# GpSimd's gate multiplications, lower parts of weights and update of x issued in pieces of 256 columns, in a two-layer token-mixer and PEER decoder on one core

## The chip, the cores and the metric

The program runs on one core of a Trainium2 chip. A core has TensorE (matrix products; PE in the profile, its weight loads PEld), VectorE (DVE), ScalarE (ACT), GpSimd (POOL) and SyncE (SP), which here issues most of the loads from device memory. Every engine works through its own list in order; semaphores tie the lists together. The metric is the device time of one execution in microseconds.

## The reference, cut to what matters

Two layers over 256 tokens of 1024 channels in float32. Each has a token mixer and a feed-forward part of single-neuron experts; both end in `layer_norm(ALPHA * x + y)`.

```python
for l in range(DEPTH):
    sh1, sc1, gt1, sh2, sc2, gt2 = jnp.split(cond @ w_ada[l] + b_ada[l], 6, axis=-1)
    hm = x * (1.0 + sc1[:, None]) + sh1[:, None]
    proj = hm @ w_in[l]                  # nine parts: q, f, i, g; q, k, v; two gates
    oa = hgrn2_chunkwise(...)            # then head norm and silu gate
    ob = stick_breaking_attention(...)
    merged = sigmoid(gate_a) * (oa @ w_up_a[l]) + sigmoid(gate_b) * (ob @ w_up_b[l])
    y = (merged @ w_o[l]) * gt1[:, None]
    x = layer_norm(DN_ALPHA * x + y, ln_g[l, 0], ln_b[l, 0])
    hf = x * (1.0 + sc2[:, None]) + sh2[:, None]
    y = peer_ffn(hf, w_pq[l], sub_keys[l], peer_u[l], peer_v[l]) * gt2[:, None]
    x = layer_norm(DN_ALPHA * x + y, ln_g[l, 1], ln_b[l, 1])
```

## The kernel before

Every float32 product is made of three products of rounded halves: a weight W is loaded into a buffer `raw` (128 x 1024, one of five), ScalarE writes its rounded upper part (tile `wh`, L58), and VectorE or GpSimd the lower part, raw minus upper part (tile `wl`, L271). TensorE forms upper x upper, upper x lower, lower x upper (L61). One load of weights is two halves of 512 columns, so two upper and two lower parts. A `raw` buffer is loaded again when its lower parts are made.

The loads stand in one list, `order`, in the order of their use, with a kind each: "w" (input and up projections), "o" (rows of w_o), "q" (queries), "u" and "x" (experts' first weights), "v" (their second). `take` fetches the next load and has one prepared ahead (`prep`); in the mixers two. Which engine makes a lower part: for u and x GpSimd; for q, and for loads prepared during a layer norm, GpSimd too (`pool_lo`); for w and o in the mixers the function `lighter`, which keeps a sum of work for each of the two engines (`load`) and gives the part to the one with less; else VectorE. Operations that GpSimd does besides are added to the sum by hand.

A mixer goes through these steps. The projections: TensorE works through w_in; between two loads a generator (`pull`) issues a piece of the side work, first `decays`, then `hgrn`, then `stick`. `hgrn` builds the scores of the HGRN2 recurrence by a binary tree of levels: for each, two subtractions on VectorE give exponents (L843, L844, tile `e`), ScalarE takes the exponential in place, two multiplications on VectorE (L856, L857, tile `qk`) give scaled keys and queries, TensorE multiplies them (tiles `hs`, `ss`), and a predicated copy (L887) places the scores. Then the second half, called the merge below: four times two up-projections on TensorE, whose results VectorE multiplies by the gates and adds (L1281 to L1283, tile `gel`), and the rows of w_o, which GpSimd multiplies by the row gt1 (tile `gt_row`, L223) when their load is near, before they are split into upper and lower part. As slabs for these parts serve tiles that the projections no longer need, so parts of w_o carry names such as `qT`, `kk`, `gaT`, `qk`. The layer norm and the first loads of the next stage follow.

In layer 1 the side work has one more member, `update_x`: x was left without the scale and shift of the last layer norm, and GpSimd applies them (L698 and L702) while the projections run. In the expert stage the same is done for the other norm, in sixteen operations of 256 columns in blocks (L1737).

Of the kernel before, what the change touches and what calls it, by code (L numbers as in the profile page):

```python
# [8 lines left out]
F32 = mybir.dt.float32  # L9
# [36 lines left out]
def trunk_kernel(ctx: ExitStack, tc: tile.TileContext, x, c, w_ada, b_ada, w_in, lb_logits, hg_norm_g,  # L46
                 w_up_a, w_up_b, w_o, w_pq, sub_keys, peer_u, peer_v, ln_g, ln_b, out):
    nc = tc.nc
# [8 lines left out]
    def act(o, i, f, **kw):  # L57
        nc.scalar.activation(o, i, f, **kw)  # L58
# [143 lines left out]
    state = {}  # L202
    xt = [const.tile([P, D], F32, name=f"x{tt}") for tt in range(2)]
    live, used = [], []
    load = {"vector": 0.0, "pool": 0.0}

    def lighter(vector, pool):

        if load["pool"] + pool < load["vector"] + vector:
            load["pool"] += pool  # L210
            return nc.gpsimd
        load["vector"] += vector
        return nc.vector

    def turn(n):

        for i in range(min(n, len(fetched))):
            kind, t = fetched[i]
            if kind == "u":
                nc.vector.transpose(t, t)  # L220
                fetched[i] = ("ut", t)
            elif kind == "o" and state.get("gt_row") is not None:
                nc.gpsimd.tensor_mul(t, t, state["gt_row"])  # L223
                load["pool"] += 2.4
                fetched[i] = ("ot", t)

    def prep():


        turn(1)  # L230
        kind, t = fetched[0]
        kind = kind[0]
        if kind in "mk":
            fetched.popleft()
            prepped.append((kind, t, None, None))
            return True
        place = room_for(kind)
        if not place:
            return False
        fetched.popleft()  # L240
        live.append(place)
        hs, ls = [], []
        if kind == "v" and state.get("vprep"):
            state["vprep"]()
        banks = []
        if kind == "x":

            for s in range(2):
                banks.append(pst.tile([P, 4, P], F32, name="T"))
                for q in range(4):  # L250
                    nc.tensor.transpose(banks[s][:, q], t[:, (4 * s + q) * P:(4 * s + q + 1) * P], ident)  # L251
        for s in range(2):
            h = place.tile([P, 512], F32R, name="wh")
            lo = place.tile([P, 512], F32R, name="wl")
            hs.append(h)
            ls.append(lo)
            if kind == "u":
                src = t.rearrange("p (a k r) -> p a k r", a=4, k=KC)[:, :, 4 * s:4 * s + 4]
                h, lo = (a.rearrange("p (k a r) -> p a k r", k=4, a=4) for a in (h, lo))
            else:  # L260
                src = t[:, s * 512:(s + 1) * 512]
            if kind == "x":
                act(h, banks[s].rearrange("p k r -> p (k r)"), AF.Copy)
                act(src, banks[s].rearrange("p k r -> p (k r)"), AF.Copy)
            else:
                act(h, src, AF.Copy)
            if kind in "ux" or state.get("pool_lo"):
                eng = nc.vector if s and state.get("share_lo") else nc.gpsimd
            else:
                eng = lighter(0.6, 1.0) if kind == "o" or kind == "w" and not state.get("slab") else nc.vector  # L270
            eng.tensor_sub(lo, src, h.bitcast(F32))  # L271
        h, lo = halves(hs), halves(ls)
        prepped.append((kind, h, lo, place))
        return True
# [10 lines left out]
    def room_for(kind):  # L285


        more = [state["more"]] if state.get("more") and not live.count(state["more"]) else []
        if kind == "w" and more:
            return more[0]  # L290
        if state.get("slab"):
            slab = state["slab"](kind)
            if slab:
                return slab
        if kind == "o" and more:
            return more[0]
        return hlp if live.count(hlp) < HALVES // 2 else None

    def halves(tiles):
        return lambda sl: tiles[sl.start // 512][:, sl.start % 512:(sl.stop - 1) % 512 + 1]  # L300

    def take(kind):
        if state.get("skip"):
            state["skip"] -= 1
        else:
            fetch()
        if kind not in "mk":
            for e in load:
                load[e] = max(0.0, load[e] - STEP)
        while used and not state.get("hold"):  # L310
            live.remove(used.pop())
        if not prepped:
            prep()
        k, h, lo, place = prepped.popleft()
        assert k == kind, (k, kind)
        if place:
            used.append(place)
        while state.get("ahead", True) and fetched and sum(p[0] not in "mk" for p in prepped) < state.get("depth", 1):
            if not prep():
                break  # L320
        turn(1 if kind in "ux" else 3)
        return h, lo
# [110 lines left out]
    def load_row(dst, src):  # L433
        nc.gpsimd.dma_start(dst, bass.AP(tensor=src.tensor, offset=src.offset, ap=[[0, P], [1, D]]))
# [36 lines left out]
    class Ahead:  # L471
# [27 lines left out]
        def others(self):  # L499

            self.tile(1, loads=range(2))
            for _ in range(2):
                live.remove(used.pop(-3))
            state["hold"] = False
            while prep():
                pass
            self.tile(1, loads=range(2, 4))
# [148 lines left out]
    def mixers(l, hT):  # L656
        with ExitStack() as es:
            ap = es.enter_context(tc.tile_pool(name=f"at{l}", bufs=1))
            psj = es.enter_context(tc.tile_pool(name=f"psj{l}", bufs=4, space=PSUM))
            gt_row = ap.tile([P, D], F32, name="gt_row")  # L660
# [29 lines left out]
            def update_x():  # L690

                g_row = ap.tile([P, D], F32, name="mh0")
                b_row = ap.tile([P, D], F32, name="mh1")
                load_row(g_row, ln_g[l - 1, 1])
                load_row(b_row, ln_b[l - 1, 1])
                yield None
                for tt in range(2):
                    nc.gpsimd.tensor_mul(xt[tt], xt[tt], g_row)  # L698
                    load["pool"] += 2.4
                    yield None  # L700
                    yield None
                    nc.gpsimd.tensor_add(xt[tt], xt[tt], b_row)  # L702
                    load["pool"] += 2.4
                    yield None
                    yield None

            if l == 0:
# [517 lines left out]
            if l:  # L1225
                sides.append(update_x())
# [35 lines left out]
            for i in range(4):  # L1262
                pp = []
                for oh, ol, n in ((oah, oal, "T"), (obh, obl, "A")):
                    h, lo = take("w")
# [529 lines left out]
```

## Time and profile before

| | |
|---|---|
| median of 3 runs | 2228.16 us (2227.01 to 2228.52) |
| the profiled execution | 2227.97 us, its span 2226.2 us |
| TensorE busy | 2117.0 us, 95% |
| VectorE busy | 1819.4 us, 82% |
| ScalarE busy | 1164.5 us, 52% |
| GpSimd busy | 1063.8 us, 48% |
| mean granted TensorE clock | 0.985 |

Busy shares are averages over the whole span. Each layer has a mixer (0 to about 310 us, 1123 to about 1400 us), the experts' first weights (to 770 and 1862 us) and the experts' second weights. A time in the rows below is counted from the start of the span.

### The profile page before, as it was taken

How to read it: one execution, taken by the hardware profiler on the slowest of the kernel's cores; microseconds unless marked ns; L12 is line 12 of the kernel's file. 1: busy time of each engine (PE TensorE's matmuls, PEld its weight loads, DVE VectorE, ACT ScalarE, POOL GpSimd, SP SyncE). 2: the span in 40 equal slices, each digit the busy share in tenths (PEclk: the TensorE clock that was granted, in tenths of full speed). 3: DMA queues.
4: the chain of work that ended last, by engine and by line, in shares of the span. 5: the costliest groups of instructions: out<-in, count | busy, mean ns of one | idle time of the engine just before them, and what ended most of it. 6: DMA issues, size and time to landing. Idle time of an engine off the chain costs nothing.

```text
span 2226.2 us, 42039 instructions
## 1 busy us (share of the span) xinstructions
PE 2117.0 (95%) x14484; PEld 1928.0 (87%) x14484; DVE 1819.4 (82%) x3296; ACT 1164.5 (52%) x2443; POOL 1063.8 (48%) x784
## 2 busy tenths in 40 slices
PE   5799899999999999999989998998999999999998
PEld 5789799999999977888779887998999999788886
DVE  7887979999999578888887658789999985766675
ACT  3446555545554545555545465555555545555562
POOL 4656637887778621000044534578877783300001
PEclk8899999999999999999999999999999999999999
DMA  8646567676665678888844335676766556666662
GB/s 281 193 133 221 167 132 158 149 151 146 143 147 146 186 251 270 282 283 284 298 153 146 120 103 146 149 155 142 154 146 145 147 159 192 220 196 191 197 226 87
DMA packets 448718, 400.30 MB, mean 180 GB/s; under 512 B 234576, under 2 KB 395896, under 8 KB 448504
## 3 DMA queue, kind: packets, MB, share of 16 engines
q1 hardware_dynamic: 446760, 392.33, 62.5%
q0 software_dynamic: 1408, 4.23, 0.6%
q8 instruction: 114, 1.87, 0.3%
q10 hardware_dynamic: 336, 1.06, 0.1%
q14 instruction: 100, 0.82, 0.1%
HBM read 396.46 MB, written 1.05 MB: 179 GB/s over the span
## 4 chain that ended last, share of the span: by engine, by line
PE 69%; DVE 15%; DMA 5%; issue 3%; ACT 3%; POOL 2%; SPq 1%; POOLq 0%; ACTq 0%; DVEq 0%
PE Y L61 27%; PE A L61 25%; PE T L61 7%; PE G L61 3%; DMA raw<-in_peer_u_dram 3%; POOL wl L271 2%; PE hs L61 2%; DVE wl L271 2%; PE ss L61 2%; PE T L251 2%; DMA raw<-in_peer_v_dram 1%; DVE qk L857 1%; DVE o L1512 1%; SPq L197 1%; DVE e L843 1%
## 5 line engine op out<-in xcount | busy, mean ns | idle before, releaser
L271 POOL TENSOR_TENSOR wl<-raw,wh 128x512 fp32r<-128x512 f32 x663 | 925.7, 1421 | 662.0 <-ACT wh L58 587.3
L58 ACT ACTIVATE wh<-raw 128x512 fp32r<-128x512 f32 x1088 | 627.7, 622 | 206.8 <-PE A L61 59.0
L61 PE MATMUL A<-hTh,wh 128*128 128x256 f32 x2080 | 538.5, 291 | 2.7 <-ACT wh L58 2.6
L61 PE MATMUL A<-hTl,wh 128*128 128x256 f32 x2080 | 521.0, 283 | 0.0
L61 PE MATMUL Y<-wh,o 128*128 128x512 f32 x1776 | 478.1, 391 | 0.5 <-DVE o L521 0.5
L271 DVE TENSOR_TENSOR wl<-raw,wh 128x512 fp32r<-128x512 f32 x525 | 379.7, 764 | 64.0 <-ACT wh L58 46.4
L61 PEld LDWEIGHTS A<-hTh,wh 128*128 128x128 f32 x2080 | 397.8, 191 | 4.7 <-ACT wh L58 4.0
L61 PEld LDWEIGHTS A<-hTl,wh 128*128 128x128 f32 x2080 | 398.7, 192 | 0.7
L61 PEld LDWEIGHTS Y<-wh,o 128*128 128x128 f32 x1776 | 332.6, 188 | 70.0 <-DVE o L521 0.9
L61 PE MATMUL A<-hTh,wl 128*128 128x256 f32 x2080 | 336.2, 284 | 13.5 <-POOL wl L271 13.4
L61 PEld LDWEIGHTS A<-hTh,wl 128*128 128x128 f32 x2080 | 286.9, 192 | 17.6 <-POOL wl L271 17.6
L61 PE MATMUL Y<-wl,o 128*128 128x512 f32 x888 | 276.3, 391 | 5.2 <-DVE wl L271 5.0
L220 DVE STREAM_TRANSPOSE raw<-raw 128x1024 f32<-128x1024 f32 x206 | 252.8, 1233 | 3.2 <-DMA raw<-in_peer_u_dram 2.7
L58 ACT ACTIVATE o<-buf 128x256 fp32r<-128x256 f32 x228 | 95.0, 417 | 272.6 <-PE Y L61 272.6
L521 DVE TENSOR_TENSOR o<-buf,o 128x256 fp32r<-128x256 f32 x228 | 100.7, 442 | 140.2 <-ACT o L58 140.2
L61 PEld LDWEIGHTS Y<-wl,o 128*128 128x128 f32 x888 | 167.1, 188 | 44.0 <-DVE wl L271 9.5
L58 ACT ACTIVATE buf<-G 128x128 f32<-128x128 f32 (+6 forms) x236 | 53.8, 273 | 202.7 <-PE G L61 202.7
L1507 DVE TENSOR_TENSOR o<-iT,iota_t 128x1024 f16<-128x1024 f16 x128 | 159.5, 1246 | 0.0
L570 POOL TENSOR_TENSOR x<-x,buf 128x1024 f32<-128x1024 f32 x1 | 2.4, 2392 | 280.9 <-DVE x L567 280.9
L1512 DVE TENSOR_TENSOR o<-gT,o 128x1024 f16<-128x1024 f16 x128 | 131.3, 1025 | 4.4
L61 PE MATMUL T<-hTh,wh 128*128 128x256 f32 x512 | 133.8, 293 | 0.0
L61 PE MATMUL T<-hTl,wh 128*128 128x256 f32 x512 | 130.4, 287 | 0.0
(496 smaller groups left out, 3212.6 us busy)
## 6 DMA issues: line engine op xcount, KB each, us to landing
raw<-in_peer_u_dram SPq DMA_DIRECT2D x1024, 128.0 KB, 3.5
raw<-in_peer_v_dram SPq DMA_DIRECT2D x256, 512.0 KB, 4.6
raw<-in_w_in_dram SPq DMA_DIRECT2D x88, 512.0 KB, 4.7
raw<-in_w_ada_dram SPq DMA_DIRECT2D x78, 512.0 KB, 4.9
raw<-in_w_o_dram SPq DMA_DIRECT2D x16, 512.0 KB, 3.5
raw<-in_w_pq_dram SPq DMA_DIRECT2D x64, 128.0 KB, 2.9
qk<-in_w_ada_dram SPq DMA_DIRECT2D x10, 512.0 KB, 3.7
e<-in_w_ada_dram SPq DMA_DIRECT2D x8, 512.0 KB, 6.0
```

The source lines that it names most:

```text
L58: nc.scalar.activation(o, i, f, **kw)
L61: nc.tensor.matmul(o, a, b, start=start, stop=stop, **kw)
L197: nc.sync.dma_start(dst[32 * b:32 * b + 32], src[b])
L220: nc.vector.transpose(t, t)
L251: nc.tensor.transpose(banks[s][:, q], t[:, (4 * s + q) * P:(4 * s + q + 1) * P], ident)
L271: eng.tensor_sub(lo, src, h.bitcast(F32))
L521: nc.vector.tensor_sub(lo, src, h.bitcast(F32))
L570: nc.gpsimd.tensor_mul(xt[tt], xt[tt], last[0])
L843: eng.tensor_sub(ev[:, :, :hn], mid, bv[:, :, :hn])
L857: nc.vector.tensor_mul(tv[:, :, hn:], nodes(qT, n)[:, :, hn:], ev[:, :, hn:])
L1507: nc.vector.tensor_tensor(o.rearrange("p a u n v -> p (a u) n v"), iT[:, b].rearrange("p a (u v) -> p (a u) v", v=2)[:, :, None] .to_broad ...
L1512: nc.vector.tensor_mul(og.rearrange("p u a n v -> p (u a) n v"), gT[:, b * nu:(b + 1) * nu].rearrange("p u a v -> p (u a) v")[:, :, None] ...
```

## The change

It issues three kinds of GpSimd operations in pieces of 256 columns, and changes the numbers by which they enter the balance:

```diff
             elif kind == "o" and state.get("gt_row") is not None:
-                nc.gpsimd.tensor_mul(t, t, state["gt_row"])
-                load["pool"] += 2.4
+                for c in range(0, 1024, 256):
+                    nc.gpsimd.tensor_mul(t[:, c:c + 256], t[:, c:c + 256], state["gt_row"][:, c:c + 256])
+                load["pool"] += 2.9
...
-            eng.tensor_sub(lo, src, h.bitcast(F32))
+            if kind not in "ux" and eng is nc.gpsimd:
+
+                for c in (slice(0, 256), slice(256, 512)):
+                    eng.tensor_sub(lo[:, c], src[:, c], h[:, c].bitcast(F32))
+            else:
+                eng.tensor_sub(lo, src, h.bitcast(F32))
...
-                for tt in range(2):
-                    nc.gpsimd.tensor_mul(xt[tt], xt[tt], g_row)
-                    load["pool"] += 2.4
-                    yield None
-                    yield None
-                    nc.gpsimd.tensor_add(xt[tt], xt[tt], b_row)
-                    load["pool"] += 2.4
-                    yield None
+                for n in range(16):
+                    cs = slice(n % 4 * 256, n % 4 * 256 + 256)
+                    xc = xt[n // 8][:, cs]
+                    (nc.gpsimd.tensor_add if n // 4 % 2 else nc.gpsimd.tensor_mul)(
+                        xc, xc, (b_row if n // 4 % 2 else g_row)[:, cs])
+                    load["pool"] += 0.7
                     yield None
```

A lower part becomes two operations, a gate multiplication four, and the four operations of `update_x` sixteen, one for each pull, where before one operation had two pulls. The lower parts of u and x stay whole. Lists of TensorE, ScalarE and SyncE are the same as before.

GpSimd, merge of layer 0, before (`raw<-raw,gt_row` is a gate multiplication, the others are lower parts of w_o):

```order
L223 TENSOR_TENSOR raw<-raw,gt_row 128x1024
L271 TENSOR_TENSOR qT<-raw,qT 128x512
L223 TENSOR_TENSOR raw<-raw,gt_row 128x1024
L271 TENSOR_TENSOR kbT<-raw,kbT 128x512
L223 TENSOR_TENSOR raw<-raw,gt_row 128x1024
L271 TENSOR_TENSOR v_b<-raw,v_b 128x512
L223 TENSOR_TENSOR raw<-raw,gt_row 128x1024 x2
L271 TENSOR_TENSOR bb<-raw,bb 128x512
L223 TENSOR_TENSOR raw<-raw,gt_row 128x1024 x3
L271 TENSOR_TENSOR qk<-raw,qk 128x512
L271 TENSOR_TENSOR wl<-raw,wh 128x512
```

The same place in the changed kernel (its lines are up to six further down):

```order
L224 TENSOR_TENSOR raw<-raw,gt_row 128x256 x4
L275 TENSOR_TENSOR qT<-raw,qT 128x256 x2
L224 TENSOR_TENSOR raw<-raw,gt_row 128x256 x4
L275 TENSOR_TENSOR kbT<-raw,kbT 128x256 x2
L224 TENSOR_TENSOR raw<-raw,gt_row 128x256 x4
L275 TENSOR_TENSOR v_b<-raw,v_b 128x256 x2
L224 TENSOR_TENSOR raw<-raw,gt_row 128x256 x12
L275 TENSOR_TENSOR sc_2490<-raw,sc_2490 128x256 x2
L224 TENSOR_TENSOR raw<-raw,gt_row 128x256 x8
L275 TENSOR_TENSOR wl<-raw,wh 128x256 x2
```

Besides the sizes, the lower parts `bb` and `qk` have gone to VectorE and `sc` has come to GpSimd; layer 1 reads the same.

GpSimd, layer 1, where the tree begins (the two MEMSETs clear its score tiles; `x_80<-x_80,mh` is the update of x by the shift row), in the changed kernel:

```order
L829 MEMSET sc_14493 128x1024
L830 MEMSET sc_14494 128x512
L275 TENSOR_TENSOR wl<-raw,wh 128x256 x4
L706 TENSOR_TENSOR x_80<-x_80,mh_13988 128x256
L275 TENSOR_TENSOR wl<-raw,wh 128x256 x2
L706 TENSOR_TENSOR x_80<-x_80,mh_13988 128x256
L275 TENSOR_TENSOR wl<-raw,wh 128x256 x4
L706 TENSOR_TENSOR x_80<-x_80,mh_13988 128x256
L275 TENSOR_TENSOR wl<-raw,wh 128x256 x4
L706 TENSOR_TENSOR x_80<-x_80,mh_13988 128x256
L275 TENSOR_TENSOR wl<-raw,wh 128x256 x72
```

Before, the four updates stood ahead of the MEMSETs, and 43 lower parts of 512 columns followed them without a break. Ahead of this place VectorE has four lower parts less in layer 1 and GpSimd four more.

## Rows read from the trace of the kernel before

**Rows 1.** Windows: length, busy us (x instructions) of PE, PEld, DVE, ACT, POOL.

```profile
80.00:235.00 155.00, 142.17 (x1005) 130.13 (x1003) 120.46 (x129) 85.06 (x147) 101.60 (x69) 0.97 0.58 185
235.00:285.00 50.00, 43.77 (x260) 38.24 (x261) 47.67 (x57) 26.72 (x47) 27.61 (x13) 0.90 0.54 153
...
1160.00:1335.00 175.00, 162.47 (x1211) 152.16 (x1211) 113.07 (x153) 92.59 (x161) 86.82 (x62) 0.98 0.41 127
1335.00:1390.00 55.00, 47.31 (x267) 40.64 (x266) 49.38 (x63) 28.81 (x54) 26.38 (x15) 0.94 0.58 151
```

**Rows 2.** Chain that ended last, one level in layer 1: start, us, what.

```profile
1225.26 1.79 DVE qk L857
1227.05 1.68 DVE e L843
1228.73 0.61 DVE e L844
...
1229.43 1.07 ACT e L58
...
1231.13 1.79 DVE qk L857
```

**Rows 3.** Waits, 112 to 152 us, then 1212 to 1252 us: total, times, longest.

```profile
PE hs L61 <- DVE qk L857: 4.4, 5, 1.3
...
PE hs L61 <- DVE qk L857: 5.8, 6, 1.1
```

**Rows 4.** Line L857: durations in ns, least, median, most.

```profile
L857 DVE TENSOR_TENSOR qk<-qT,e x16: 679/1788/1802, 109.0 to 1248.7; 128x512 f32<-128x512 f32 x16
```

**Rows 5.** Timeline of GpSimd: start, us, operation.

```profile
279.73 1.37 POOL L271 TENSOR_TENSOR wl<-raw,wh 128x512 fp32r<-128x512 f32 x1 [0.32 <-POOL qk L271]
...
295.04 1.30 POOL L271 TENSOR_TENSOR qbT<-raw,qbT 128x512 fp32r<-128x512 f32 x1
...
1225.22 2.96 POOL L271 TENSOR_TENSOR wl<-raw,wh 128x512 fp32r<-128x512 f32 x2 [2.90 <-ACT wh L58]
```

**Rows 6.** Lines L223 and L1737: durations in ns, first and last start.

```profile
L223 POOL TENSOR_TENSOR raw<-raw,gt_row x16: 2378/2760/2871, 232.3 to 1363.6; 128x1024 f32<-128x1024 f32 x16
...
L1737 POOL TENSOR_TENSOR x<-x,buf x32: 709/916/1717, 822.0 to 1929.0; 128x256 f32<-128x256 f32 x32
```

**Rows 7.** Timeline, merge of layer 1.

```profile
1341.22 2.38 POOL L223 TENSOR_TENSOR raw<-raw,gt_row 128x1024 f32<-128x1024 f32 x1
1341.26 2.89 DVE L1283 TENSOR_TENSOR gel<-gel,mgb 128x512 f32<-128x512 f32 x1
```

**Rows 8.** Groups by form, VectorE, 239.5 to 281 and 1335 to 1376 us.

```profile
L271 DVE TENSOR_TENSOR wl<-raw,wh 128x512 fp32r<-128x512 f32 x13 | 18.9, 1498 | 0.3 <-ACT wh L58 0.3
L1283 DVE TENSOR_TENSOR gel<-gel,mgb 128x512 f32<-128x512 f32 x4 | 4.8, 1191 | 0.1
...
L271 DVE TENSOR_TENSOR wl<-raw,wh 128x512 fp32r<-128x512 f32 x12 | 14.2, 1226 | 0.0
L1283 DVE TENSOR_TENSOR gel<-gel,mgb 128x512 f32<-128x512 f32 x4 | 8.1, 2014 | 0.1
```

**Rows 9.** Waits of TensorE, 239 to 282 us, then 1333 to 1377 us.

```profile
PE T L61 <- DVE wl L271: 2.4, 2, 1.8
...
PE T L61 <- DVE wl L271: 4.9, 2, 2.8
```

**Rows 10.** Timeline of VectorE beside the 256-column updates, expert stage of layer 0.

```profile
832.73 1.22 DVE L271 TENSOR_TENSOR wl<-raw,wh 128x512 fp32r<-128x512 f32 x1
```

**Rows 11.** Timeline, start of layer 0: GpSimd, then VectorE.

```profile
54.50 6.34 POOL L271 TENSOR_TENSOR wl<-raw,wh 128x512 fp32r<-128x512 f32 x5
...
54.59 1.26 DVE L682 TENSOR_SCALAR m_a<-iota_f,part_f 128x8 f32<-128x8 f32 x1
```

**Rows 12.** Timeline, expert stage of layer 0: VectorE, then GpSimd.

```profile
821.02 4.26 DVE L271 TENSOR_TENSOR wl<-raw,wh 128x512 fp32r<-128x512 f32 x2
...
821.96 2.77 POOL L1737 TENSOR_TENSOR x<-x,buf 128x256 f32<-128x256 f32 x4
```

## The prediction

> **What bounds the kernel now.** I looked first at the stretches. Outside the start and the token mixers TensorE hardly stops; in the mixers it does. The four rows of [rows 1] are the two halves of each layer's mixer: TensorE is idle for 155.0 − 142.2 = 12.8 us and 50.0 − 43.8 = 6.2 us in layer 0, 175.0 − 162.5 = 12.5 us and 55.0 − 47.3 = 7.7 us in layer 1. Of the change's parts nearly all stand there (the parts of the expert weights, kinds u and x, keep their 512 columns), so about 39 us of idle TensorE is what there is to win, and a longer VectorE or GpSimd path is what there is to lose.
>
> Next the chain of waits. In the first half it runs through VectorE level after level of the HGRN2 tree: [rows 2] is one level, 5.87 us from one multiplication L857 to the next, of which ScalarE's exponential has 1.07 and VectorE the rest. TensorE waits for that L857: 4.4 us over levels in layer 0, 5.8 us in layer 1 [rows 3]. Why VectorE is slow there shows in the durations: L857 takes 679 ns at its shortest and 1788 ns as a rule [rows 4]. It starts at 1225.26; GpSimd started a pair of lower parts at 1225.22 [rows 5]. The first 512 columns of GpSimd hold L857 for 1.79 − 0.68 = 1.11 us; the second half of the pair holds L843, which takes 1.68 us of the chain where the unheld L844 takes 0.61, so 1.07 us. The two engines take turns: GpSimd, VectorE, GpSimd, VectorE.
>
> In the second half (up-projections, merge, w_o) the longest holders are the multiplications by the gate row: 2378 ns at their shortest [rows 6], and a VectorE operation that comes 0.04 us behind one takes 2.89 us [rows 7]. There VectorE's lower parts and the last addition of the merge are on average far above 0.68 us [rows 8], and TensorE waits for its lower parts for 2.4 us in layer 0 and 4.9 us in layer 1 [rows 9].
>
> **The price of a piece.** The trace has the new form already: the update of x in the expert stage is issued in 256 columns. Alone it takes 0.709 us [rows 6]; its median beside VectorE's lower parts is 0.916, and a 512-column operation of VectorE that meets one takes 1.22 us [rows 10], which is a whole turn of both engines. So a piece holds VectorE for 1.22 − 0.68 = 0.54 us where 512 columns hold it for 1.1 and 1024 for 2.2. Undisturbed, a pair of pieces costs GpSimd 2 × 0.71 = 1.42 us against 1.30 for 512 columns [rows 5]; I take 0.12 us as what one more instruction costs. The changed program has 173 lower parts in 350 pieces, 16 gate multiplications in 64 and 4 updates of x in 16, 237 instructions more, so some 28 us more of GpSimd, spread over an engine that is idle more than half of the time.
>
> A rule that speaks against the change: the Trainium skill, GPSIMD Engine Reference, section 2.1, says that every GpSimd instruction passes a dispatch in software first, tens of cycles. The 0.12 us of the rows is of that size; an estimate by the page's 1.2 GHz, with 100 cycles for its tens, is 20 us for the 237, no more than by the rows.
>
> **Levels of the tree.** In a level where VectorE then waits for the exponential, L857, L843 and L844 now meet one piece each, 3 × 0.54 = 1.62 us instead of 1.11 + 1.07 = 2.18; the fourth piece runs while VectorE waits for ScalarE. That is 0.56 us a level. By the chain ten levels end that way, four in layer 0 and six in layer 1: 5.6 us. Four others in layer 0 have further VectorE work behind L844 (accumulating weights, reducing); there all four pieces are paid, 4 × 0.54 = 2.16 for 2.18, nothing. The last level of each layer is held once before TensorE's products: 2 × (1.11 − 0.54) = 1.1 us. TensorE's waits of 4.4 and 5.8 us have room for it.
>
> Against it: the update of x in layer 1 went out in four operations before the tree; now the last four of its sixteen pieces stand between the tree's first lower parts. Each can hold VectorE once more: nothing to 2.2 us. I take half, −1.1, since two of them fall behind L844, where VectorE waits for ScalarE anyway. Levels together: +5.6 us (bounds +2 to +8).
>
> **Merge.** Each of the four waits of [rows 9] (2.4 us in two, the longer 1.8; 4.9 in two, the longer 2.8) stands behind a hold by a whole gate multiplication, 2.2 us; held by a piece it is 0.54, so each can shrink by 1.67: 1.67 + 0.6 in layer 0, 1.67 + 1.67 in layer 1, 5.6 us. What comes back: the balancing gives VectorE one lower part more in each layer (two gained, one lost), 2 × 0.61; and the last lower part on GpSimd, which the last w_o products need, comes in two pieces, 2 × 0.2. Left: about +4 us. The bounds are wide. VectorE's whole excess over 0.68 us is 13 × 0.82 + 4 × 0.51 = 12.7 us in layer 0 and 12 × 0.55 + 4 × 1.33 = 11.9 in layer 1 [rows 8], yet TensorE's idle time caps it at 6.2 and 7.7; from the other side a multiplication whose four pieces all collide takes 4 × 1.22 = 4.9 us against the median 2.76 [rows 6], and ScalarE's rounding of w_o waits for it. So −5 to +9, and I stay near the middle, by the waits that the rows show.
>
> **Start of layer 0, and the hand-overs.** Here I expect nothing. At 54.5 us five lower parts follow each other and hold five small VectorE operations, each 1.2 to 1.3 us instead of 0.2 [rows 11]. In pieces they hold ten by half as much, and the VectorE work behind is long enough to meet all ten. The same holds for the decays around 92 us. GpSimd's later end delays a buffer's release by one 0.12 us. Bounds −1 to +1.
>
> **Sum.** 5.6 + 4 − 0.1 = 9.5 us off the profiled execution's 2227.97 us, which is 0.2 us below the median of the runs (2228.16): 2218.5 us.
>
> **Rivals.** *The port time is the same.* GpSimd holds VectorE for a time that goes by the columns it works on, and they are as many as before. Where VectorE has enough work behind the first held operation, as in [rows 11], it pays every column anyway. If that held in the ten levels and the merge too, only the two last levels would gain, 1.1 us, less the 1.2 of the extra lower parts: 2228 us, no change. The Trainium skill, SBUF — State Buffer, "two separate sides", states the mechanism: an exclusive lock, held for a whole instruction; the trace agrees in that L857 waits for the end of an operation, 1.11 us. Against the rival: VectorE's pause for ScalarE in each level, 1.07 us, in which a piece costs nothing. Chance 0.2.
>
> *GpSimd becomes the bound of the merge (slower).* In layer 0 its first gate multiplication begins at 232.3 us [rows 6] and its last lower part ends at 281.1 [rows 5]; into these 49 us go 32 + 18 = 50 pieces, 35.5 us alone and 0.51 more for each that collides (1.22 less 0.71). From 27 collisions on GpSimd would be late, from 32 on by more than the levels bring (2.8 us a layer); VectorE has about 30 lower parts, last additions and the like there that can be held. At 40 it is late by 7 us a layer: 14 less 5.6, 2236 us. For it: w_o's rounding waits for the multiplications. Against: GpSimd is idle half of these stretches [rows 1]. Chance 0.1.
>
> *VectorE isn't let in between pieces (slower).* Once a VectorE lower part stayed out until four pieces had passed one behind the other: two of them took 4.26 us where 1.28 would do, with 2.77 us of pieces beside it [rows 12]. In the levels four pieces in one block hold L857 for 2.8 us instead of two holds of 2.18 together, 0.6 × 10 = 6 us, and the merge brings nothing: 2234 us. Against: that one came right behind a DMA issue of GpSimd, and [rows 10] shows the engines taking turns on the same form a dozen us later. Chance 0.05.
>
> *More than forecast.* If the merge gives back two thirds of TensorE's 13.9 idle us there, 9.3, and the pieces of x cost nothing: 2212 us. Chance 0.2. The forecast itself, 2214 to 2222, has 0.45.
>
> **Numbers.** A measurement of this kernel tells about 0.2%, 4.5 us, from no change. Faster by more: 0.45 + 0.2 = 0.65; within: 0.2; slower: 0.15. The range reaches over the first rival and the start of the slower ones and down past the larger gain: 2208 to 2232, which leaves out some 0.1 above and 0.05 below.
>
> **What would show it.** Right: L857, L843 and L844 at about 1.2 us each in place of 1.79, 1.75 and 0.68, the levels some 5.3 us apart, TensorE's wait for L857 about halved; no VectorE operation of the merge above about 1.4 us; gate pieces between 0.7 and 1.2 us. Wrong: levels still 5.87 us apart (the port's time is the same); VectorE operations of 2.5 us and more beside rows of pieces (not let in); ScalarE's rounding of w_o or TensorE's products waiting for gate pieces (GpSimd the bound). What would make the number wrong though the mechanism is right is the merge, whose term has the widest bounds.

## The result, and the profile after

The changed kernel takes 2213.11 us (median of 4 runs, 2211.72 to 2214.66) against 2227.75 us for the kernel before on the same chip (4 runs): a ratio of 0.9934, 95% interval 0.9917 to 0.9952, so 14.6 us off with some 4 us either way. The forecast was 9.5 us off. The profiled execution has a span of 2210.5 us against 2226.2, 15.7 us less.

The engines' busy time on the page, to be read beside the table of before: TensorE does the same work, GpSimd 91 us more where the working had some 28, VectorE 39 us less (a held operation counts as busy for as long as it is held).

```profile
PE 2116.5 (96%) x14484; PEld 1925.0 (87%) x14484; DVE 1780.7 (81%) x3294; ACT 1164.5 (53%) x2443; POOL 1155.3 (52%) x1021
```

A level of layer 1's tree in the timeline of the changed kernel, VectorE and then GpSimd (start us, us, operation), the answer to [rows 2, 5]:

```profile
1211.95 0.69 DVE L860 TENSOR_TENSOR qk<-kk,e 128x512 f32<-128x512 f32 x1 [0.49 <-ACT e L58]
1212.57 1.25 DVE L861 TENSOR_TENSOR qk<-qT,e 128x512 f32<-128x512 f32 x1
1213.74 1.21 DVE L847 TENSOR_TENSOR e<-bb 128x512 f32<-128x512 f32 x1
1214.87 1.21 DVE L848 TENSOR_TENSOR e<-bb 128x512 f32<-128x512 f32 x1
...
1217.27 0.69 DVE L860 TENSOR_TENSOR qk<-kk,e 128x512 f32<-128x512 f32 x1 [0.50 <-ACT e L58]
...
1212.52 4.16 POOL L275 TENSOR_TENSOR wl<-raw,wh 128x256 fp32r<-128x256 f32 x4 [0.46 <-ACT wh L58]
```

Four pieces begin at 1212.52. Three VectorE operations meet one each, 1.25, 1.21 and 1.21 us; the fourth piece runs while VectorE waits for the exponential. The levels are 1217.27 − 1211.95 = 5.32 us apart instead of 5.87. TensorE's waits for the second multiplication, over levels in layer 0 and in layer 1 (total, times, longest), against 4.4 and 5.8 us in [rows 3]:

```profile
PE hs L61 <- DVE qk L861: 1.6, 3, 0.7
...
PE hs L61 <- DVE qk L861: 2.6, 5, 0.6
```

The gate pieces, least, median and most in ns, beside the whole ones of [rows 6]:

```profile
L224 POOL TENSOR_TENSOR raw<-raw,gt_row x64: 718/1183/1266, 226.7 to 1356.0; 128x256 f32<-128x256 f32 x64
```

In the merges VectorE's lower parts are now at 1.03 us instead of 1.50 in layer 0 [rows 8], and none of its operations takes above 1.24 us:

```profile
L277 DVE TENSOR_TENSOR wl<-raw,wh 128x512 fp32r<-128x512 f32 x17 | 16.9, 1033 | 2.7 <-ACT wh L58 2.6
L527 DVE TENSOR_TENSOR acc<-gel,mh 128x512 fp32r<-128x512 f32 x4 | 4.8, 1198 | 0.7 <-ACT mh L58 0.7
```

**Where the time came from.** TensorE's list is the same in all these kernels, 14,484 products, so the n-th product of one trace can be set beside the n-th of another. The table gives how many us earlier than before TensorE leaves a stretch, less how many it entered it earlier; the stretches are bounded by the products that start nearest behind 80, 232, 300, 1124, 1150, 1172, 1255, 1335 and 1390 us in the trace of before. The first column counts from the start of the span, the last is the whole up to the last product. The lines behind the first are the experiments below.

```
                               start layer0 merge0 experts norm masks tree1 stick1 merge1 rest   all
                                0-80 80-232    -300  -1124 -1150 -1172 -1255 -1335  -1390
changed kernel                  1.8    4.3    0.7    2.2    0.9   2.5   3.0  -0.2   -0.1   0.5  15.7
e1 lower parts alone            1.1    4.3    0.8    0.6    1.2   0.3   4.9   0.0   -0.8  -0.2  12.2
e2 gates alone                 -0.8    0.1    1.0    0.6    0.0   0.0  -0.9   0.0    2.6   0.2   2.9
e3 update of x alone           -0.4   -0.5    0.7    0.5    0.0   0.4  -3.3   0.0    0.0   0.3  -2.2
e4 all but the gates            1.9    3.7    0.7    3.0    1.2   2.3   3.3   0.0    0.0   0.8  16.9
e5 w_o's lower parts on DVE     0.9    4.3    3.0    2.3    0.9   2.8   4.0  -0.4    1.7   0.6  20.2
e5b w_o's lower parts whole     1.9    4.0    1.6    0.7    0.9   3.5   4.0  -0.2    1.5   0.8  18.6
e6 lower parts in 128           4.0   -8.0   -0.9    1.8    1.5   5.4  -0.7  -0.5   -2.2   0.6   1.3
e7 row loads by SyncE           1.2    4.2    0.2    1.5    0.9   1.6   2.0  -0.2   -0.7   0.7  11.3
e8 as e5, gates whole           0.9    4.0    0.6    2.1    1.1   2.3   3.3  -1.9    1.7   0.8  15.0
e9 as e5, gates on DVE          0.7    4.3    5.4    3.2    1.2   2.7   2.7  -0.3    4.6   0.6  25.2
e10 gates on DVE, parts shared  1.5    4.1    4.0    2.7    1.2   2.7   2.6  -0.3    2.7   0.6  21.9
e11 as e9, all parts on DVE     1.6   -2.0    2.4    1.4    1.2   5.0   2.8   0.0    4.4   0.5  17.2
```

Where two kernels have the same instructions in a stretch, the column shows the scatter of one execution: e2 and e3 differ from before by up to 0.8 us at the start, the kernels with lower parts in pieces lie between 0.6 and 3.2 us over the 820 us of the experts. Nor do the other columns repeat to a tenth: e1 and e4, alike in all of layer 0, differ by 0.6 us in its tree, and e3, which is the kernel before in all of layer 0, shows 0.7 us in its merge. So a difference below 1 us says little by itself, and in the experts' column one of 2.4 says nothing.

The merges are the surprise: of the 15.7 us, they hold 0.6 us, and the 0.7 of layer 0 is no more than e3 shows there without a change. TensorE is 10.9 us early by 274 us, against 6.1 us where the merge begins, and has given 4.1 of the 4.8 us back by 300 us; in layer 1 it gains 5.7 us and gives 5.8 back. The end of the merge of layer 0 in the timeline of the changed kernel, GpSimd and then ScalarE:

```profile
266.37 6.47 POOL L224 TENSOR_TENSOR raw<-raw,gt_row 128x256 f32<-128x256 f32 x6
273.58 1.87 POOL L275 TENSOR_TENSOR wl<-raw,wh 128x256 fp32r<-128x256 f32 x2 [0.74 <-ACT wh L58]
...
270.60 0.63 ACT L58 ACTIVATE wh<-raw 128x512 fp32r<-128x512 f32 x1 [1.64 <-POOL raw L224]
272.87 2.71 ACT L58 ACTIVATE wh<-raw 128x512 fp32r<-128x512 f32 x5 [1.64 <-POOL raw L224]
```

GpSimd works on gate pieces up to 272.84; ScalarE rounds the last rows of w_o when they are through, and TensorE's last products need these. ScalarE's waits for gate multiplications over this merge (230 to 277 us: total, times, longest) add up to 7.7 us; in the kernel before they are 0.2 us:

```profile
ACT wh L58 <- POOL raw L224: 3.3, 2, 1.6
...
ACT sc L58 <- POOL raw L224: 1.6, 1, 1.6
ACT gaT L58 <- POOL raw L224: 1.4, 1, 1.4
ACT v_b L58 <- POOL raw L224: 0.8, 1, 0.8
ACT e L58 <- POOL raw L224: 0.6, 1, 0.6
```

### The profile page after: what moved, and what is told of

It reads as the page before. It is cut to its first block, busy times and chain, and to the rows that moved or that the text cites. A ratio compares the mean times of both kernels' runs of the same rounds, so it can differ in the third digit from the quotient of the medians.

```text
span 2210.5 us, 42352 instructions
## 1 busy us (share of the span) xinstructions
PE 2116.5 (96%) x14484; PEld 1925.0 (87%) x14484; DVE 1780.7 (81%) x3294; ACT 1164.5 (53%) x2443; POOL 1155.3 (52%) x1021
## 5 line engine op out<-in xcount | busy, mean ns | idle before, releaser
L277 POOL TENSOR_TENSOR wl<-raw,wh 128x512 fp32r<-128x512 f32 x512 | 713.5, 1420 | 199.7 <-ACT wh L58 135.5
L275 POOL TENSOR_TENSOR wl<-raw,wh 128x256 fp32r<-128x256 f32 x310 | 272.7, 912 | 388.2 <-ACT wh L58 382.8
L277 DVE TENSOR_TENSOR wl<-raw,wh 128x512 fp32r<-128x512 f32 x521 | 371.2, 752 | 73.1 <-ACT wh L58 55.0
```

The costliest lines, as they stand in the source:

```text
L275: eng.tensor_sub(lo[:, c], src[:, c], h[:, c].bitcast(F32))
```

## The experiments

The theory after the two traces: a GpSimd operation keeps VectorE out for its own length; pieces halve that wherever VectorE has a short chain, in the start, the norms and the masks too, not in the trees alone; in the merges GpSimd itself becomes what TensorE waits for. The rivals: the gain outside the trees is the scatter of one execution; the merges end where they do for another reason (loads, or the sum of both engines' work).

**e1 to e3, one part alone; e4, all but the gates.** Each is the kernel before with the named parts of the diff: e1 the lower parts, e2 the gate multiplications (with the 2.9), e3 the update of x, e4 the lower parts and the update of x. The kernel before was measured again beside each group of experiments; its medians lie between 2227.06 and 2228.45 us, so medians of different groups can be compared to some 1.4 us.

> Only the lower parts in pieces; gate multiplications and the update of x whole, as before. Theory 1 (every VectorE operation that a lower part holds is held half as long, in the trees and in the start, the masks and the layer norms too): TensorE comes out of the two trees 4.3 and 3.1 us earlier or a little more, out of the start some 1.8 us earlier, out of the experts' hand-overs and the layer norm ahead of layer 1 some 2 to 3 us earlier; about 11 us off in all. Theory 2 (as forecast: only the trees gain, and what the changed kernel shows at the start and the hand-overs is the scatter of one profiled execution): 6 to 7 us off.

Measured: 2215.13 us (5 runs), ratio 0.9944 (0.9930 to 0.9958), 12.6 us off. The first theory holds: start, norm and tree of layer 1 gain 1.1, 1.2 and 4.9 us.

> Only the gate multiplications in pieces. Only the two merges can differ. Theory 1 (GpSimd is the bound of the end of the merge: in the changed kernel it works without a pause from 249.3 to 272.8 us, a gate multiplication in four pieces takes 4.7 us instead of 2.85, and the last roundings of w_o wait for it): TensorE is some 4 us earlier in the middle of each merge and has given nearly all of it back at its end; 0 to 2 us off in all. Theory 2 (as forecast, each wait for a lower part behind a gate multiplication shrinks and the end follows): 4 us off.

Measured: 2223.35 us (11 runs), ratio 0.9982 (0.9973 to 0.9991), 4.4 us off. Here the forecast's 4 us stand, and the first theory's "0 to 2" does not: alone, the gate pieces bring 1.0 and 2.6 us in the two merges (of the 1.0, e3's 0.7 may be scatter). It was too coarse: what the gates bring depends on whether GpSimd's lower parts are in pieces as well.

> Only the update of x in layer 1 in sixteen pieces. Theory 1 (the whole operations hold the small mask operations of VectorE for about 2.2 us each, and these stand in one chain ahead of the lower parts that TensorE waits for; the pieces go elsewhere): TensorE's wait for VectorE's lower part at the masks shrinks from 4.9 us by 1.5 to 2.5 us, the pieces that fall into the tree take back up to 1 us; 1 to 2 us off. Theory 2 (as forecast): nothing gained at the masks, the tree some 1 us longer; 1 us slower.

Measured: 2231.22 us (11 runs), ratio 1.0014 (1.0005 to 1.0023), 3.5 us slower. Neither size is right; the direction is the forecast's. Beside whole lower parts nearly nothing is gained at the masks (0.4 us), and the pieces that fall into the tree cost 3.3 us.

> Lower parts and the update of x in pieces, the gate multiplications whole: the changed kernel less its gate pieces. Theory 1 (the gate pieces give back at the merge's end what they gain in its middle): as fast as the changed kernel within 1.5 us, 13 to 16 us off the kernel before. Theory 2 (as forecast, the gate pieces bring 4 us): 9 to 11 us off.

Measured: 2211.58 us (5 runs), ratio 0.9928 (0.9915 to 0.9942), 16.1 us off, as fast as the changed kernel or a little faster. Given the other two parts, the gate pieces bring nothing. In e4 ScalarE waits for no gate multiplication, but TensorE waits 4.6 us for VectorE's lower parts (230 to 280 us), which are held by whole multiplications again: one wait in the place of the other. From e1 to e4 the update of x in pieces brings 2.0 us at the masks and costs 1.6 in the tree; the rest of what lies between their traces stands mostly in start and experts of layer 0, where the two kernels have the same instructions. Scatter of one execution is not all of it, though: their medians are 3.5 us apart, and each run of e4 is faster than each of e1. What the rest is stays open.

**e5, e5b, e8: who is the bound of the merge.** In e5 GpSimd makes no lower part of a gated row of w_o; in e5b it makes them whole; e8 is e5 with the gate multiplications whole.

```diff
-                eng = lighter(0.6, 1.0) if kind == "o" or kind == "w" and not state.get("slab") else nc.vector
+                eng = nc.vector if kind == "o" and state.get("gt_row") is not None else lighter(0.6, 1.0) if kind == "o" or kind == "w" and not state.get("slab") else nc.vector
```

```diff
-            if kind not in "ux" and eng is nc.gpsimd:
+            if kind not in "uxo" and eng is nc.gpsimd:
```

> The changed kernel, but VectorE makes all lower parts of w_o behind the gate multiplications, GpSimd has only the gate pieces there. Theory 1 (GpSimd's row of pieces is what the end of the merge waits for: in the changed kernel ScalarE waits 7.7 us for gate pieces in the merge of layer 0): that wait falls to 3 us or less, the 4.1 and 5.8 us that TensorE gives back at the two merge ends become 1 to 2, and the kernel is 2 to 6 us faster than the changed one, about 2209 us. Theory 2 (the two engines share one path to the buffers, and the sum of their work bounds the merge, whoever does it): VectorE's five lower parts more in each layer, at 0.68 us, come in the place of GpSimd's, and nothing is gained: 2213 us within 1.5.

Measured: 2206.35 us (4 runs), ratio 0.9907 (0.9892 to 0.9922), 6.8 us faster than the changed kernel, somewhat more than the first theory's 2 to 6. The five lower parts are dearer on GpSimd than on VectorE. At their ends the merges give back 1.0 us in layer 0, as expected, but 2.7 in layer 1; ScalarE's waits for gate pieces fall to 3.9 us, a little more than expected.

> The changed kernel, but the lower parts of w_o on GpSimd whole (512 columns), the gate multiplications in pieces. With whole lower parts everywhere the gate pieces alone brought TensorE 1.0 us in the merge of layer 0 and 2.6 us in that of layer 1; in the changed kernel the merges brought 0.7 and nothing. Theory 1 (each collision of a piece with a VectorE operation costs GpSimd 0.5 us, and five lower parts in ten pieces make it late by some 2 us at the end of each merge): the merges as with the gate pieces alone, 2 to 3 us faster than the changed kernel, about 2211 us. Theory 2 (the difference is scatter of one execution): as the changed kernel, 2213 us.

Measured: 2209.35 us (5 runs), ratio 0.9926 (0.9913 to 0.9940), 3.8 us faster than the changed kernel, with 1.6 and 1.5 us from the merges: the first theory.

> As the run in which VectorE makes all lower parts of w_o, but with the gate multiplications whole. Theory 1 (with no lower parts to make there, GpSimd has time for the slower row of pieces, and now the shorter hold of a piece pays: VectorE is held 0.5 us by a piece, 2.2 us by a whole multiplication): TensorE's waits for VectorE's lower parts come back to 4 us and more a merge, and the kernel is 2 to 5 us slower than with the pieces, about 2209 to 2211 us. Theory 2 (what that run gained came from the lower parts' place alone): as fast as it, 2206 us within 1.5.

Measured: 2212.92 us (5 runs), ratio 0.9931 (0.9917 to 0.9944), 6.6 us slower than e5: the first theory, stronger than its 2 to 5 us. With GpSimd relieved, the gate pieces do pay. In layer 0 the merge itself loses 2.4 us. In layer 1 1.5 us are lost ahead of it, where the first gate multiplications go out beside the end of the attention: VectorE, then GpSimd, in e8's timeline:

```profile
1314.46 2.30 DVE L986 TENSOR_TENSOR sb_w<-sb_w,strict 128x256 f32<-128x256 f32 x1
...
1314.12 2.35 POOL L223 TENSOR_TENSOR raw<-raw,gt_row 128x1024 f32<-128x1024 f32 x1 [1.32 <-DMA raw<-in_w_o_dram]
```

The whole multiplication holds to 2.30 us an operation that takes 0.41 us at its shortest, and TensorE waits 1.4 us for it.

**e6, pieces of 128 columns.**

```diff
-                for c in (slice(0, 256), slice(256, 512)):
+                for c in (slice(n, n + 128) for n in range(0, 512, 128)):
```

> The changed kernel with its lower parts in pieces of 128 columns (gates and update of x in 256). Theory 1 (a piece holds one VectorE operation for its own length, 0.54 us at 256 columns, so about 0.27 at 128): L861, L847 and L848 take about 0.95 us in a level instead of 1.21, levels are 4.5 to 4.8 us apart instead of 5.3, ten levels give 5 to 8 us, and the start and the layer norms some 2 us; the merges lose up to 3; 2205 to 2210 us. Theory 2 (the hold goes by the columns GpSimd works on, since eight pieces now meet every VectorE operation of a level, and each piece has a fixed part): levels stay 5.3 us apart and the merges lose 2 to 4: 2215 to 2217 us.

Measured: 2227.14 us (11 runs), ratio 1.0006 (0.9997 to 1.0015): as slow as the kernel before, slower than either theory. The hold does shrink, VectorE's rows in a level (1208 to 1213 us), and this level has 4.79 us to the next:

```profile
1208.13 0.98 DVE L860 TENSOR_TENSOR qk<-kk,e 128x512 f32<-128x512 f32 x1 [1.12 <-ACT e L58]
1209.04 0.94 DVE L861 TENSOR_TENSOR qk<-qT,e 128x512 f32<-128x512 f32 x1
1209.91 0.94 DVE L847 TENSOR_TENSOR e<-bb 128x512 f32<-128x512 f32 x1
1210.77 0.94 DVE L848 TENSOR_TENSOR e<-bb 128x512 f32<-128x512 f32 x1
1212.92 0.76 DVE L860 TENSOR_TENSOR qk<-kk,e 128x512 f32<-128x512 f32 x1 [1.21 <-ACT e L58]
```

Two things cost more than that brings. GpSimd hardly keeps up: over 80 to 230 us it is busy for 136 us of 150, and TensorE waits longer for its lower parts (80 to 120 us, total, times, longest; in the changed kernel the second row has 2.5 us and the first is not there):

```profile
PE T L61 <- ACT v_a L58: 8.0, 1, 8.0
PE T L61 <- POOL wl L275: 4.0, 6, 1.3
```

The first row is another matter. VectorE, then GpSimd, in e6's timeline (x64 is 64 pieces without a pause between them):

```profile
72.18 1.28 DVE L387 SCALAR_TENSOR_TENSOR acc<-raw,cond,acc 128x1024 f32<-128x1024 f32 x1 [1.43 <-DMA raw<-in_w_ada_dram]
81.63 13.77 DVE L387 SCALAR_TENSOR_TENSOR acc<-raw,cond,acc 128x1024 f32<-128x1024 f32 x1 [8.17 <-DMA raw<-in_w_ada_dram]
...
65.01 29.31 POOL L275 TENSOR_TENSOR wl<-raw,wh 128x128 fp32r<-128x128 f32 x64 [1.39 <-PE hs L61]
```

An accumulation that takes 1.28 us elsewhere began beside this row and ended only when the row was through; the pieces passed at 0.50 us each. Its `raw` buffer came free late: SyncE waited 10.7 us for it to issue the next load, ScalarE 10.7 us for that load, TensorE 8.0 us for ScalarE. Around this wait TensorE falls from 3.1 us early to 6.8 late; that is 9.9 of the 12.3 us that lie between e6 and the changed kernel in layer 0's tree (−8.0 against 4.3). This is one trace; whether the other ten runs have the same hold isn't known.

**e7, the DMA issue.** At three places of the changed kernel one VectorE operation was out for longer than a piece, each time beside a DMA issue of GpSimd: twice a lower part in the expert stages (3.67 and 3.50 us), and here, at the masks of layer 1, VectorE and then GpSimd:

```profile
1148.54 3.03 DVE L688 TENSOR_SCALAR m_a<-iota_f,part_f 128x8 f32<-128x8 f32 x1
1149.16 2.42 DVE L689 TENSOR_SCALAR m_b<-iota_f,part_f 128x8 f32<-128x8 f32 x1
...
1148.28 0.59 POOL L440 DMA_DIRECT2D mh<-in_ln_g_dram  x1
1148.86 0.53 POOL L440 DMA_DIRECT2D mh<-in_ln_b_dram  x1
1149.41 2.83 POOL L275 TENSOR_TENSOR wl<-raw,wh 128x256 fp32r<-128x256 f32 x4
```

The same two operations take 0.23 us each some us later. The edit lets SyncE issue the two loads:

```diff
-                load_row(g_row, ln_g[l - 1, 1])
-                load_row(b_row, ln_b[l - 1, 1])
+                for dst, src in ((g_row, ln_g[l - 1, 1]), (b_row, ln_b[l - 1, 1])):
+                    nc.sync.dma_start(dst, bass.AP(tensor=src.tensor, offset=src.offset, ap=[[0, P], [1, D]]))
```

> The changed kernel with the two loads of rows for the update of x in layer 1 issued by SyncE instead of GpSimd. In the changed kernel a small VectorE mask operation that began 0.3 us ahead of GpSimd's second issue took 3.03 us, until four pieces behind that issue were nearly through. Theory 1 (a VectorE operation that meets a DMA issue of GpSimd stays out until the queue behind it has passed): without the issue no mask operation takes above 0.8 us, TensorE's wait for VectorE's lower part at the masks (2.4 us) falls to 1 us or less, 1 to 2 us off in all: 2211 to 2212 us. Theory 2 (it is the four pieces standing ready in a row that keep VectorE out, not the issue): the long operation stays, and nothing is gained.

Measured: 2213.59 us (5 runs), ratio 0.9940 (0.9926 to 0.9954): no gain. The long operation is gone from the masks, as the first theory says (both now stay below 0.8 us):

```profile
1150.90 0.75 DVE L688 TENSOR_SCALAR m_a<-iota_f,part_f 128x8 f32<-128x8 f32 x1
1151.57 0.78 DVE L689 TENSOR_SCALAR m_b<-iota_f,part_f 128x8 f32<-128x8 f32 x1
```

Yet TensorE's wait at the masks is 3.3 us instead of 2.4 (in a profiled execution that is the slowest of the five, 2216.49 us). Without the long hold, more of the small operations of this chain meet a piece, one each and some 0.5 us each; the four pieces that had passed under one hold now meet four operations. In this chain of small operations VectorE pays for GpSimd's columns either way.

**e9 to e11: GpSimd's work given to VectorE.** e9 is e5 with the gate multiplications on VectorE, e10 the changed kernel with them there, e11 is e9 with the lower parts of the projections on VectorE too.

```diff
-                for c in range(0, 1024, 256):
-                    nc.gpsimd.tensor_mul(t[:, c:c + 256], t[:, c:c + 256], state["gt_row"][:, c:c + 256])
-                load["pool"] += 2.9
+                nc.vector.tensor_mul(t, t, state["gt_row"])
+                load["vector"] += 1.3
```

> VectorE makes all lower parts of w_o and the gate multiplications too, whole; GpSimd has nothing in the merges but the lower parts during the layer norms. Theory 1 (a GpSimd operation holds VectorE longer than VectorE would need for the same columns: four pieces 4 x 0.54 = 2.16 us, one VectorE operation of 1024 columns some 1.2 us): VectorE's time in a merge falls by up to 6 us, no operation of it there takes above 1.3 us, and the kernel is 1 to 4 us faster than with the gate pieces on GpSimd: 2202 to 2205 us. Theory 2 (VectorE is then the bound of the merge, and its lower parts stand behind multiplications that wait for their loads): 3 us slower or more, 2209 us and above.

Measured: 2203.28 us (4 runs), ratio 0.9892 (0.9876 to 0.9907): the fastest of all, 24.1 us below the kernel before of the same session and 9.8 below the changed one. 5.4 and 4.6 us come from the merges. VectorE's groups in the merge of layer 0 (230 to 277 us):

```profile
L276 DVE TENSOR_TENSOR wl<-raw,wh 128x512 fp32r<-128x512 f32 x18 | 11.5, 687 | 0.4 <-ACT wh L58 0.4
L223 DVE TENSOR_TENSOR raw<-raw,gt_row 128x1024 f32<-128x1024 f32 x7 | 8.5, 1220 | 0.0
```

VectorE multiplies a row by the gates in 1.22 us; GpSimd's four pieces held it for 4 × 0.54 = 2.16 us where each met an operation. And its lower parts are back at 0.69 us.

> VectorE makes the gate multiplications whole, GpSimd gets lower parts of w_o in pieces by the sums of work (eight in layer 0). Theory 1 (the hold is dear, whoever fills it): between the run with everything on VectorE and the changed kernel, 2205 to 2211 us. Theory 2 (sharing the lower parts is worth more than their holds cost): the fastest of these, 2203 us or less.

Measured: 2206.21 us (4 runs), ratio 0.9906 (0.9891 to 0.9921): the first theory, sharing costs 3 us against e9.

> As the run with the gate multiplications and w_o's lower parts on VectorE (2203.3 us), and VectorE makes the lower parts of the projections too; GpSimd keeps the update of x, the small things and the lower parts during layer norms. Theory 1 (what GpSimd does costs VectorE more than doing it itself, everywhere): levels below 5 us apart instead of 5.3, and 2 to 6 us faster: 2197 to 2201 us. Theory 2 (in a level of the tree one piece of four is hidden behind ScalarE's exponential, so three holds, 1.62 us, stand against two lower parts of 0.6 us; and VectorE's lower parts must wait for ScalarE's two roundings, 1.2 us, which stand behind the exponential, with the next multiplications queued behind them): levels 5.5 to 6.2 us apart, and 3 to 9 us slower: 2206 to 2212 us.

Measured: 2213.67 us (5 runs), ratio 0.9934 (0.9920 to 0.9947), 10 us slower than e9: the second theory, somewhat stronger. A level in the timeline, VectorE and then ScalarE:

```profile
1207.12 0.69 DVE L860 TENSOR_TENSOR qk<-qT,e 128x512 f32<-128x512 f32 x1
1207.73 0.69 DVE L846 TENSOR_TENSOR e<-bb 128x512 f32<-128x512 f32 x1
1208.33 0.69 DVE L847 TENSOR_TENSOR e<-bb 128x512 f32<-128x512 f32 x1
1210.72 1.29 DVE L276 TENSOR_TENSOR wl<-raw,wh 128x512 fp32r<-128x512 f32 x2 [1.71 <-ACT wh L58]
...
1213.20 0.69 DVE L860 TENSOR_TENSOR qk<-qT,e 128x512 f32<-128x512 f32 x1
...
1209.11 1.06 ACT L58 ACTIVATE e<-e 128x1024 f32<-128x1024 f32 x1 [2.83 <-DVE e L847]
1210.07 1.14 ACT L58 ACTIVATE wh<-raw 128x512 fp32r<-128x512 f32 x2
```

Nothing holds VectorE any more, each operation takes 0.69 us. But its lower parts stand ahead of the next multiplications and wait 1.71 us for ScalarE's roundings, which stand behind the exponential: 6.08 us a level instead of 5.32. By the table the loss against e9 stands in layer 0: 6.3 us in the tree, and 3.0 in the merge, at whose start TensorE waits 3.0 us for VectorE's end of the attention (sb_w, L986). In layer 1 the slow levels give back only 1.7 us of the 3.6 that TensorE had gained just ahead of them, and the masks, where GpSimd has no lower part any more, gain 5.0.

## Why the prediction was right, and where it was not

The time lies inside the range and the direction was right, but the sum was not: 9.5 us were forecast and 14.6 came, below the 2214 to 2222 us that had the most chance. The merge's 4 us did not come; some 9 us more than forecast came from the start, the hand-overs and the masks, which the sum had at nothing, and from the trees, which it counted short. That the time is still in the range is in part luck, as these errors have opposite signs. The rival "more than forecast" has nearly the time, 2212 us, but not for its reason: it let the merges give 9.3 us, and they gave 0.6.

**Levels of the tree: right in mechanism, a little small.** The six steps of TensorE's gain at layer 1's levels are 0.52 to 0.59 us, 3.28 together, against 0.56 forecast for each. In layer 0 the gain is 4.3 us, more than four levels and the last one. Taken from one L856 to the next in VectorE's timeline (L860 in the changed kernel), the four levels shrink by 0.55 to 0.59 us, and so do two with a reduction behind L844, costed at nothing: from 6.08 and 6.02 us to 5.52 and 5.46. The working had all four pieces paid there; but the reduction reads TensorE's products and takes 0.68 us with and without a piece beside it, so the fourth piece is free. It stands in the timelines before and after as

```profile
130.49 0.68 DVE L393 TENSOR_REDUCE mod<-A 128x4 f32<-128x512 f32 x1
```

```profile
126.57 0.68 DVE L399 TENSOR_REDUCE mod<-A 128x4 f32<-128x512 f32 x1
```

The level with an accumulation behind L844 gave 0.10, near the nothing forecast, the last hold 0.55 and what stands ahead of the first level 0.3. Both trees with their decays make 7.3 us, against 5.6.

**The pieces of x in the tree: mis-sized, with a gain elsewhere that was missed.** The term was −1.1 us. Set against e1 they cost layer 1's tree 1.9 us (4.9 to 3.0). What the working left out is their old place: beside whole updates mask operations of 0.2 us took 2.3 us each. Masks in the kernel before:

```profile
1163.74 2.32 DVE L684 TENSOR_TENSOR m_a<-m_a,m_b 128x32 f32<-128x32 f32 x1
...
1167.20 2.38 DVE L682 TENSOR_SCALAR m_a<-iota_f,part_f 128x64 f32<-128x64 f32 x1
```

With pieces TensorE's wait behind the masks falls from 4.9 to 2.4 us. By e1 and the changed kernel, that is 2.2 us gained: the part's two effects cancel.

**Merge: the step that failed.** "Each can shrink by 1.67", the working says of TensorE's waits behind a gate multiplication, and so they did: 10.5 us earlier in the middle of the two merges. What failed is the next step, that the end of the merge follows. The rival "GpSimd becomes the bound of the merge" had the mechanism, with a chance of 0.1, and put its point at 27 collisions of 50 pieces. There are 42 pieces (ten of lower parts, not 18, as the list ahead of the prediction already had it), and 28 of them take above 1.1 us. The same price is missing from the working's 28 us more of GpSimd over the whole kernel, which counts pieces undisturbed: it was 91. Over the whole merge GpSimd is busy for 44.1 us of the 48.8 from its first gate piece to its last lower part, which would leave slack; but GpSimd's pieces follow each other without a pause from 249.25 to 272.84, and there nearly every one collides: a gate multiplication takes 4.7 us instead of 2.85. The sign that the prediction had named for it, ScalarE's rounding of w_o waiting for gate pieces, is there with 7.7 us. So the rival's bound came, as a cap and not as a loss: 0.6 us instead of 4. e2 shows the 4 (4.4 us by its runs) where lower parts are whole; e5b and e5 show 3.1 and 4.7 us in the merges when those of w_o are whole or on VectorE. The waits that the term started from were not firm either: e3, with the instructions of before in layer 0, waits 4.1 us there where [rows 9] has 2.4.

**Start and hand-overs: costed at nothing, worth 4.9 us.** That is 1.8 at the start, 2.2 over the experts and 0.9 at the norm ahead of layer 1, 0.9 to 1.5 in every run with the lower parts in pieces and 0.0 in e2 and e3. (Of the 2.2 us some 0.6 are there in e2 and e3 too.) The reason given, that VectorE's work behind is long enough to meet every piece, holds only where VectorE has such work; the norm is a chain with waits for ScalarE in it. Two of its steps, before and after:

```profile
1139.75 2.36 DVE L540 SCALAR_TENSOR_TENSOR buf<-x,buf 128x256 f32<-128x256 f32 x2
...
1143.73 1.30 DVE L567 TENSOR_SCALAR x<-buf,lnmv 128x1024 f32<-128x1024 f32 x1
```

```profile
1130.98 1.31 DVE L546 SCALAR_TENSOR_TENSOR buf<-x,buf 128x256 f32<-128x256 f32 x2
...
1133.92 0.91 DVE L573 TENSOR_SCALAR x<-buf,lnmv 128x1024 f32<-128x1024 f32 x1
```

**The rivals.** That the port time is the same is refuted for the levels (0.55 us each); for a chain of small operations e7's one trace agrees with it. That VectorE isn't let in between pieces did not happen in the changed kernel's levels and merges, where it takes turns, and happened there only beside a DMA issue; in e6 it happened in plain rows of pieces and TensorE lost 9.9 us around one such hold, so as a rule the rival is not refuted. The sum of the table's first line by these parts: trees 7.3, masks 2.5, start and hand-overs 4.9, merges 0.6, the rest 0.4: 15.7 us.

What stays open is how much of the start's and the experts' gain is the pieces' and how much scatter.

## What to carry to other kernels

Cutting an engine's operation shortens what it holds on another, but each meeting costs the cut engine too, so before counting the gain ask how long its row of pieces then is and who waits for the last: here 256 columns paid and 128 did not, and the gate pieces paid beside whole lower parts (e2) or without lower parts on GpSimd (e5 against e8), but not beside lower parts in pieces (e4). A long row without a pause is a danger of its own: look for single operations of the other engine that last as long as the row (e6). Where two engines keep each other out, compare the hold with what the held engine would need for the same work itself: 2.16 us against 1.22 made the move to VectorE worth more than the pieces. But such a move pays only if the moved work's inputs are ready where it stands in the list; behind a late input it blocks the chain (e11).

## What the runs showed of the hardware

**A collision costs GpSimd as well.** A piece of 256 columns takes 0.72 to 0.75 us alone and 1.18 beside a lower part of VectorE, one of 128 columns 0.45 to 0.46 and 0.90. The Trainium skill, SBUF — State Buffer, "two separate sides", has an exclusive lock on which the loser blocks for a whole instruction. The traces agree where both engines lose in turn: 1.18 us for GpSimd and 1.22 for VectorE are a turn of both, 1.14 to 1.15 us from one start to the next. They differ where VectorE stays out for many instructions, as told below.

**Small operations are held too.** Mask operations on 4 to 64 columns take 0.76 to 0.78 us beside a piece instead of 0.22 to 0.24, but the memory sets between them stay at 0.09 us, and VectorE's operations of the merge that read TensorE's products (L1285, L1286) stay at 0.67 us beside gate pieces.

**VectorE can stay out for a whole row.** Beside a DMA issue of GpSimd it did so for 3.03 us in the changed kernel, 3.46 at the same place before, 4.26 for the two operations in [rows 12]; with the issue on SyncE no mask operation there took above 0.78 us. But the issue is neither enough nor needed. In e2 a lower part that began 0.22 us behind such an issue, at 819.73 us, took 0.69 us, and the two engines took turns from there on. In e6 two operations of 1024 columns took 13.77 and 7.49 us, beside 31 and 18 pieces, with no issue near. What decides it no run here tells.
